# Gated activations turned in 32x32 squares by VectorE and regrouped through device memory, in a two-layer encoder on one core

## The chip, the cores and the metric

The kernel runs on one core of a Trainium2 chip. The metric is device time in microseconds (us), from the program's start to its end; lower is better. The median of three runs of the kernel before is 1835.18 us (1835.18 to 1835.51).

A core has a matrix engine (TensorE, rows named PE, with its weight loads under PEld), VectorE (DVE), ScalarE (ACT), GpSimd (POOL) and SyncE (SP), each with its own in-order queue of instructions, and 16 DMA engines. An instruction waits until its operands are there, and everything behind it on the same engine waits with it. SP here does nothing but issue DMAs; a DMA that must wait, for a buffer to come free or for data to be finished, holds up the DMAs behind it on SP.

## The reference, cut to what matters

Two layers; 512 tokens of width 1024, float32. Each layer holds two gated feed-forward blocks ("ffn" below, inner width 2816) with attention and convolution ("mix") between them:

```python
def swiglu(x, w_gate, w_up, w_down):
    return (jax.nn.silu(x @ w_gate) * (x @ w_up)) @ w_down

for l in range(DEPTH):
    x = x + 0.5 * swiglu(rms_norm(x, ffn1_norm[l]), ffn1_w_gate[l], ffn1_w_up[l], ffn1_w_down[l])
    ...  # h, attention and conv from x
    x = x + jnp.concatenate([attn, conv], axis=-1) @ w_out[l]
    x = x + 0.5 * swiglu(rms_norm(x, ffn2_norm[l]), ffn2_w_gate[l], ffn2_w_up[l], ffn2_w_down[l])
    x = rms_norm(x, post_norm[l])
```

The change touches the four ffn blocks only.

## The kernel before, in words

`x` stays on the chip with its features on the 128 partitions: `x[:, m, :]` holds features 128m to 128m+127 of all 512 tokens, for m = 0 to 7. Every float32 product is made of three matmuls of rounded halves: each operand is split into a high part (an ACT cast) and a low part (a DVE subtraction), and `mm3` adds high times high, high times low and low times high in a PSUM bank (lines 144 to 146). A bank holds 128 partitions x 512 float32.

An ffn goes through its 22 tiles of 128 inner features in six units (`UNITS` = 2, 4, 4, 4, 4, 4 tiles; unit 0 is `opening`, units 1 to 5 are `unit`). A unit of four tiles makes gate and up for all 512 tokens by a Strassen scheme with seven `product` calls of 24 matmuls each, in the order b11, b21, t2, t3, t1, t4, b22 (the names of the token-side operands). The weight sums that the scheme needs are made by DVE from loaded tiles (`add`, line 325), and the weights are split by line 227 (ACT) and line 229 (DVE). The results have tokens on the partitions. They are put together by `copied` and `join` (lines 341 and 346), and `gated` makes silu(gate) times up: an ACT instruction (line 355) and a DVE instruction (line 356) per 128 tokens, each 128x256.

The second matmul of the ffn, `down`, needs the inner features on the partitions. So `turned` transposes: four 128x128 TensorE transposes against an identity fill one bank with one tile of inner features for all 512 tokens (line 365), and `split` makes its high and low part from the bank (lines 150 and 151). There are two banks of that kind for `opening` and four for each unit. The `down` matmuls (96 for four tiles) of one unit are placed between the products of the next: `between(0)` turns, `between(1)` to `between(4)` take two of the eight output tiles each. `update` (line 443) adds half the bank to `x`. The last unit's activations are turned after the first matmuls of the last `down` groups, which also take unit 4's tiles.

The order of instructions on each engine is set by a scheduler at build time, which follows the program's order and its own estimates of durations; a DMA is placed in SP's order by the same scheduler. Buffers come from pools with a fixed number of places: `fr` 9 places for loaded gate and up weights (a unit uses 8), `raw` 3 for loaded `down` weights and two weight sums, `wh` and `wl` 4 each for split weights, `e` 4 for activations, `r` 40 (the "ring") for operands on the token side, PSUM 7 banks. `POOL` issues the few DMAs that add while they load (line 317), through a scratch area whose size `dynamic_dma_scratch_size` sets.

## Time and profile before

| | |
|---|---|
| median of three runs | 1835.18 us |
| the profiled execution's own time | 1836.73 us |
| its span, first to last instruction | 1834.9 us |
| mean granted TensorE clock | 0.993 |
| PE busy | 1793.2 us, 98% |
| DVE busy | 1347.8 us, 73% |
| ACT busy | 948.6 us, 52% |
| share of the 16 DMA engines taken by SP's queue | 28.6% |
| matmuls of line 365 (transposes) | 352 |

A row of a group gives line, engine, operation, output and inputs by name, shapes, count, then busy time in us and the mean duration of one in ns, then the engine's idle time just before and what ended it. In a timeline the first column is the start in us from the span's start, the second the time until the last of the row's instructions ends. A row of the windows view gives a stretch, its length, and for each engine the busy us with the number of instructions, then the granted clock, the share of DMA time and GB/s. Matmuls overlap, so the time that one takes from the next is read from the distance of their starts and not from a duration. The transposes of line 365 mark the four ffn blocks: they lie at about 38 to 319, 593 to 874, 940 to 1228 and 1502 to 1783 us.

### The profile page before, as it was taken

How to read it: one execution, taken by the hardware profiler on the slowest of the kernel's cores; microseconds unless marked ns; L12 is line 12 of the kernel's file. 1: busy time of each engine (PE TensorE's matmuls, PEld its weight loads, DVE VectorE, ACT ScalarE, POOL GpSimd, SP SyncE). 2: the span in 40 equal slices, each digit the busy share in tenths (PEclk: the TensorE clock that was granted, in tenths of full speed). 3: DMA queues.
4: the chain of work that ended last, by engine and by line, in shares of the span. 5: the costliest groups of instructions: out<-in, count | busy, mean ns of one | idle time of the engine just before them, and what ended most of it. 6: DMA issues, size and time to landing. Idle time of an engine off the chain costs nothing.

```text
span 1834.9 us, 22168 instructions
## 1 busy us (share of the span) xinstructions
PE 1793.2 (98%) x8512; PEld 1489.1 (81%) x8512; DVE 1347.8 (73%) x1803; ACT 948.6 (52%) x1471; POOL 279.0 (15%) x216
## 2 busy tenths in 40 slices
PE   8999999999999999999998999999999999999997
PEld 6888888888788888888877888888978788888885
DVE  8957876587957957866778667755988678577754
ACT  6534445467954634445644344444778455344442
POOL 4000000058931000000000000000688300000000
PEclk9999999999999999999999999999999999999998
DMA  8332322225134332322712332123250534323221
GB/s 294 107 123 89 117 70 69 92 87 136 25 127 106 108 123 93 105 99 69 229 66 92 107 103 92 69 71 112 76 149 1 164 89 126 115 81 115 69 70 58
DMA packets 58492, 187.95 MB, mean 102 GB/s; under 512 B 6033, under 2 KB 6417, under 8 KB 58385
## 3 DMA queue, kind: packets, MB, share of 16 engines
q1 hardware_dynamic: 54496, 173.56, 28.6%
q0 software_dynamic: 3456, 12.58, 3.9%
q8 instruction: 67, 1.10, 0.3%
q10 hardware_dynamic: 432, 0.38, 0.1%
q14 instruction: 41, 0.33, 0.1%
HBM read 184.40 MB, written 2.10 MB: 102 GB/s over the span
## 4 chain that ended last, share of the span: by engine, by line
PE 69%; issue 19%; DVE 7%; ACT 3%; POOL 2%; DMA 1%; SPq 0%; POOLq 0%; DVEq 0%; ACTq 0%
PE ps L144 21%; PE ps L146 21%; PE ps L145 20%; PE ps L752 2%; PE ps L365 1%; PE ps L718 1%; DVE wl L229 1%; ACT pr L795 1%; PE ps L739 1%; DVE fr L325 1%; DVE wl L139 1%; DVE cv L791 1%; POOL y L799 1%; POOL sck L162 0%; PE ps L182 0%
## 5 line engine op out<-in xcount | busy, mean ns | idle before, releaser
L144 PE MATMUL ps<-wh,r 128*128 128x512 f32 (+2 forms) x1392 | 525.2, 387 | 13.0 <-ACT wh L227 7.5
L145 PE MATMUL ps<-wl,r 128*128 128x512 f32 (+2 forms) x1392 | 534.5, 386 | 0.0
L146 PE MATMUL ps<-wh,r 128*128 128x512 f32 (+2 forms) x1392 | 532.1, 385 | 0.0
L227 ACT CAST wh<-fr 128x1024 fp32r<-128x1024 f32 x256 | 268.9, 1050 | 264.4 <-PE ps L146 141.3
L229 DVE TENSOR_TENSOR wl<-fr,wh 128x1024 fp32r<-128x1024 f32 x256 | 314.3, 1230 | 106.0 <-ACT wh L227 105.8
L146 PE MATMUL ps<-r,wl 128*128 128x512 f32 x1008 | 391.4, 389 | 0.5 <-POOL wl L139 0.5
L145 PE MATMUL ps<-r,wh 128*128 128x512 f32 x1008 | 391.4, 389 | 0.0
L144 PE MATMUL ps<-r,wh 128*128 128x512 f32 x1008 | 390.7, 393 | 0.3 <-ACT r L150 0.3
L144 PEld LDWEIGHTS ps<-wh,r 128*128 128x128 f32 x1392 | 262.4, 189 | 63.6 <-ACT wh L227 7.5
L145 PEld LDWEIGHTS ps<-wl,r 128*128 128x128 f32 x1392 | 262.5, 189 | 50.6 <-issue 0.5
L146 PEld LDWEIGHTS ps<-wh,r 128*128 128x128 f32 x1392 | 262.4, 188 | 50.2
L133 ACT CAST wh<-raw 128x1024 fp32r<-128x1024 f32 (+2 forms) x150 | 148.9, 997 | 217.8 <-issue 89.0
L146 PEld LDWEIGHTS ps<-r,wl 128*128 128x128 f32 x1008 | 189.2, 188 | 40.9 <-POOL wl L139 1.3
L145 PEld LDWEIGHTS ps<-r,wh 128*128 128x128 f32 x1008 | 189.2, 188 | 40.6 <-issue 1.4
L144 PEld LDWEIGHTS ps<-r,wh 128*128 128x128 f32 x1008 | 188.8, 188 | 40.9 <-ACT r L150 1.2
L139 DVE TENSOR_TENSOR wl<-raw,wh 128x1024 fp32r<-128x1024 f32 (+3 forms) x134 | 157.9, 1179 | 64.1 <-ACT wh L133 63.1
L162 POOL TENSOR_TENSOR rtok<-vtok,minus_half 128x4 f32<-128x4 f32 x9 | 11.1, 1230 | 1107.7 <-DVE vtok L188 1107.7
L443 DVE SCALAR_TENSOR_TENSOR x<-ps,x 128x512 f32<-128x512 f32 x128 | 88.2, 689 | 111.4 <-PE ps L146 110.7
L799 POOL TENSOR_TENSOR y<-y,pr 128x509 f32<-128x509 f32 (+15 forms) x120 | 157.7, 1316 | 50.2 <-ACT pr L795 42.9
L325 DVE TENSOR_TENSOR fr<-fr,fr 128x1024 f32<-128x1024 f32 x112 | 135.3, 1219 | 7.7 <-DMA fr<-in_wgu 7.2
L355 ACT ACTIVATE e<-e,rtok 128x256 f32<-128x256 f32 x120 | 61.0, 509 | 111.5 <-DVE e L346 111.2
L341 ACT COPY e<-ps 128x512 f32<-128x512 f32 x120 | 70.3, 587 | 64.1 <-PE ps L146 63.9
(165 smaller groups left out, 1731.9 us busy)
## 6 DMA issues: line engine op xcount, KB each, us to landing
fr<-in_wgu SPq DMA_DIRECT2D x176, 512.0 KB, 4.0
raw<-in_wd SPq DMA_DIRECT2D x64, 512.0 KB, 4.2
raw<-in_wd SPq DMA_DIRECT2D x32, 384.0 KB, 3.2
raw<-in_wcv SPq DMA_DIRECT2D x16, 512.0 KB, 3.3
raw<-in_wout SPq DMA_DIRECT2D x16, 512.0 KB, 3.7
raw<-in_wgu SPq DMA_DIRECT2D x8, 512.0 KB, 4.2
fr<-in_wgu POOLq DMA_DIRECT2D x8, 512.0 KB, 7.0
raw<-in_wgu POOLq DMA_DIRECT2D x8, 512.0 KB, 7.6
```

The lines of the kernel that those rows point to most:

```text
L133: A.copy(hi[:, :w], raw[:, :w])
L139: (G if kind in POOLW.split() else V).tensor_tensor(lo[:, :w], raw[:, :w], hi[:, :w].bitcast(FP), ALU.subtract)
L144: T.matmul(o, lh, rh, start=first, stop=False, skip_group_check=free)
L145: T.matmul(o, lh, rl, start=False, stop=False, skip_group_check=free)
L146: T.matmul(o, ll, rh, start=False, stop=last, skip_group_check=free)
L227: A.copy(hi[:, :w], src[:, :w])
L229: V.tensor_tensor(lo[:, :w], src[:, :w], hi[:, :w].bitcast(FP), ALU.subtract)
L325: V.tensor_tensor(oh, ah, bh, ALU.add)
L341: A.copy(w[:, j, :N], o[j][:, :N])
L355: A.activation(out[j][:, :h], src[j][:, :h], AF.Silu, scale=r)
L443: V.scalar_tensor_tensor(x[:, m, :], pd, 0.5, x[:, m, :], ALU.mult, ALU.add)
L799: order["conv"] = G.tensor_tensor(acc[:, s:], acc[:, s:], pr[:, s:], ALU.add).ins
```

## The change

The transposes on TensorE go away. What `gated` leaves, 128 tokens x 256 inner features, is turned by VectorE in squares of 32x32 (`turn`): one instruction takes a 128x256 tile and writes 128 x 8 x 32 into a block of 128 x 8 x 128. After it, partition 32a + i of the block holds, for each of eight groups of 32 inner features, feature i of the group for the 32 tokens of the a-th quarter of each 128. Two tiles of inner features for all 512 tokens fill one block, by four such instructions. `moved` then writes the block to device memory with four DMAs, one for each a (32 partitions, 256 runs of 512 bytes, 128 KB), and reads it back with two DMAs of 256 KB, one for each tile of inner features. The tokens of the tile that comes back stand in the order a, t, j instead of t, a, j. `down` works on them as they stand, and `update` reads its bank in the permuted order (t, a, j) to add it to `x`. The factor 0.5 of `update` is now in `rh`, half of the norm's factor, which `gated` multiplies in. `halved` makes the high part by an ACT cast from the tile read, and the low part in place by DVE.

A unit's blocks are moved in the order b1, b0, so the two halves of a unit's four tiles swap places, and the host puts the rows of the `down` weights in that order (`turns`). `moved` is called at the end of the unit in the program, `halved` where `turned` stood. `e` gets five places instead of four, the pool of one R tile one instead of two, and the scratch area is halved.

```diff
-WIDE = 4
+WIDE = 5
...
-    rpool = ctx.enter_context(tc.tile_pool(name="rp", bufs=2))
+    rpool = ctx.enter_context(tc.tile_pool(name="rp", bufs=1))
+    dram = ctx.enter_context(tc.tile_pool(name="dram", bufs=4, space=bass.MemoryType.DRAM))
...
         def gated(t, src, out, N):
             h = N // 2
             for j in range(2):
-                r = rt[0][:, 2 * t + j:2 * t + j + 1]
+                r, rh = (v[:, 2 * t + j:2 * t + j + 1] for v in rt)
                 A.activation(out[j][:, :h], src[j][:, :h], AF.Silu, scale=r)
-                V.scalar_tensor_tensor(out[j][:, :h], src[j][:, h:N], r, out[j][:, :h], ALU.mult, ALU.mult)
+                V.scalar_tensor_tensor(out[j][:, :h], src[j][:, h:N], rh, out[j][:, :h], ALU.mult, ALU.mult)
             return out
-        def turned(vs, N, act):
-            for b in range(len(vs)):
-                for i in range(N // 2 // P):
-                    ps = bank()
-                    for t in range(2):
-                        for j in range(2):
-                            T.transpose(ps[:, (2 * t + j) * P:(2 * t + j + 1) * P],
-                                        vs[b][t][j][:, i * P:(i + 1) * P], ident)
-                    act.append(split(ps))
+        def block():
+            return fpool.tile([P, 8, P], FP, tag="e", name=nm("e"), bufs=WIDE)
+
+        def turn(to, t, v):
+            for j in range(2):
+                V.transpose(to[:, :, (2 * t + j) * 32:(2 * t + j + 1) * 32], v[j][:, :HS])
+
+        def moved(blk):
+            away = dram.tile([2, P, S], FP, tag="d", name=nm("d"))
+            for a in range(4):
+                nc.sync.dma_start(
+                    out=away[:, :, a * P:(a + 1) * P].rearrange("f (b i) t -> i (f b) t", i=32),
+                    in_=blk[a * 32:(a + 1) * 32])
+            ds = []
+            for i in range(2):
+                d = slot(FR)
+                nc.sync.dma_start(out=d.bitcast(FP), in_=away[i])
+                ds.append(d)
+            return ds
+
+        def halved(d):
+            hi = slot(FR)
+            A.copy(hi, d.bitcast(FP))
+            V.tensor_tensor(d, d.bitcast(FP), hi.bitcast(FP), ALU.subtract)
+            return hi, d
...
         # opening
-            rt.append(norm())
-            vs = []
+            rt.extend((norm(), tiny("rh", NT)))
+            V.tensor_scalar(rt[1], rt[0], 0.5, None, ALU.mult)
+            blk = block()
             for t in range(2):
-                v = wide()
-                vs.append(gated(t, os[2 * t:2 * t + 2], [v[:, j, 0:HS] for j in range(2)], S))
-            return [vs]
+                v = tmp()
+                turn(blk, t, gated(t, os[2 * t:2 * t + 2], [v[:, j * HS:(j + 1) * HS] for j in range(2)], S))
+            return moved(blk)
...
         # unit
-            gated(0, a, a, N)
+            b0 = block()
+            turn(b0, 0, gated(0, a, a, N))
...
-            gated(1, d, d, N)
+            b1 = block()
+            turn(b1, 1, gated(1, d, d, N))
...
-            gated(0, c, c, N)
+            turn(b1, 0, gated(0, c, c, N))
+            b1 = moved(b1)
             product(bx, a12, "b22", False, True)
             s = tmp()
-            s = gated(1, bx, [s[:, j * HS:(j + 1) * HS] for j in range(2)], N)
-            return [[a, s], [c, d]]
+            turn(b0, 1, gated(1, bx, [s[:, j * HS:(j + 1) * HS] for j in range(2)], N))
+            return b1 + moved(b0)
 
         def update(m, pd):
-            V.scalar_tensor_tensor(x[:, m, :], pd, 0.5, x[:, m, :], ALU.mult, ALU.add)
+            xm = x[:, m, :].rearrange("p (t a j) -> p t a j", t=NT, a=4)
+            V.tensor_tensor(xm, pd.rearrange("p (a t j) -> p t a j", a=4, t=NT), xm, ALU.add)
...
                 if i == 0:
-                    turned(vs, S, acts)
+                    acts.extend(halved(d) for d in ds)
...
+    turns = np.arange(F).reshape(NF, P)
+    for f in range(UNITS[0], NF, 4):
+        turns[f:f + 4] = turns[[f + 2, f + 3, f, f + 1]]
...
-    nc = bacc.Bacc("TRN2", target_bir_lowering=False, num_devices=1, dynamic_dma_scratch_size=4096)
+    nc = bacc.Bacc("TRN2", target_bir_lowering=False, num_devices=1, dynamic_dma_scratch_size=2048)
```

How the order moves is shown at three places. In the rows below, line numbers of the changed kernel differ from those of the kernel before by one to a few tens, and the number behind a name tells tiles of one pool apart.

First DVE, at the passage from unit 3 to unit 4 of the first ffn, from the gating of c (e_1417, in the change e_1434) to the split of the first weight of product t2 (wl_1847, in the change wl_1868). Before, with the last gating instructions of unit 3 (line 356) between splits and sums of unit 4's weights:

```order
L356 SCALAR_TENSOR_TENSOR e_1417<-e_1417,rtok_326 128x256
L356 SCALAR_TENSOR_TENSOR t_1669<-ps_1232,rtok_326,t_1669 128x256
L325 TENSOR_TENSOR fr_1676<-fr_1676,fr_1684 128x1024
L229 TENSOR_TENSOR wl_1769<-fr_1678,wh_1767 128x1024
L356 SCALAR_TENSOR_TENSOR t_1669<-ps_1233,rtok_326,t_1669 128x256
L229 TENSOR_TENSOR wl_1773<-fr_1680,wh_1771 128x1024
L325 TENSOR_TENSOR fr_1678<-fr_1678,fr_1674 128x1024
L325 TENSOR_TENSOR fr_1680<-fr_1680,fr_1676 128x1024
L139 TENSOR_TENSOR wl_1809<-raw_1805,wh_1807 128x1024
L229 TENSOR_TENSOR wl_1847<-fr_1674,wh_1845 128x1024
L151 TENSOR_TENSOR r_1735<-ps_1729,r_1734 128x512
```

The same place in the change, without its first rows:

```order
L326 TENSOR_TENSOR fr_1718<-fr_1718,fr_1726 128x1024
L230 TENSOR_TENSOR wl_1787<-fr_1720,wh_1785 128x1024
L366 STREAM_TRANSPOSE e_1578<-e_1434 128x8x32
L366 STREAM_TRANSPOSE e_1395<-t_1700 128x8x32
L357 SCALAR_TENSOR_TENSOR t_1700<-ps_1271,rh_330,t_1700 128x256
L230 TENSOR_TENSOR wl_1791<-fr_1722,wh_1789 128x1024
L326 TENSOR_TENSOR fr_1720<-fr_1720,fr_1716 128x1024
L366 STREAM_TRANSPOSE e_1395<-t_1700 128x8x32
L140 TENSOR_TENSOR wl_1827<-raw_1823,wh_1825 128x1024
L326 TENSOR_TENSOR fr_1722<-fr_1722,fr_1718 128x1024
L230 TENSOR_TENSOR wl_1868<-fr_1716,wh_1866 128x1024
L230 TENSOR_TENSOR wl_1872<-fr_1718,wh_1870 128x1024
```

The transposes of unit 3 stand among the splits that unit 4's first products need, and the second split for t2 has moved up next to the first.

Second SP, at the same passage. Before, it has loads alone:

```order
L315 DMA fr_1682<-in_wgu 128x1024
L315 DMA fr_1684<-in_wgu 128x1024
L131 DMA raw_1805<-in_wd 128x2x512
L315 DMA fr_1686<-in_wgu 128x1024
L315 DMA fr_1688<-in_wgu 128x1024
L315 DMA fr_2134<-in_wgu 128x1024
L131 DMA raw_1880<-in_wd 128x2x512
L315 DMA fr_2136<-in_wgu 128x1024
```

In the change:

```order
L316 DMA fr_1730<-in_wgu 128x1024
L316 DMA fr_2180<-in_wgu 128x1024
L372 DMA d_1659<-e_1578 32x8x128 x4
L378 DMA r_1664<-d_1659 128x512
L378 DMA r_1666<-d_1659 128x512
L372 DMA d_1707<-e_1395 32x8x128 x4
L132 DMA raw_1901<-in_wd 128x2x512
L316 DMA fr_2182<-in_wgu 128x1024
L378 DMA r_1712<-d_1707 128x512
L378 DMA r_1714<-d_1707 128x512
L316 DMA fr_2184<-in_wgu 128x1024
```

The writes of the blocks (d) and the reads of the tiles (r) stand in the one queue with the weight loads; the reads of the second block stand behind a load of `down` weights and the second load for unit 5 (fr_2182).

Third PE, at the end of the first ffn, where unit 5's activations are taken. Before, after the twelve matmuls of the third output tile (ps_2478) on unit 4's activations:

```order
L146 MATMUL ps_2478<-r_2221,wl_2474 128x512
L365 MATMUL ps_2515<-cst,e_2186 128x128 x2
L365 MATMUL ps_2515<-cst,t_2453 128x128 x2
L365 MATMUL ps_2524<-cst,e_2186 128x128 x2
L365 MATMUL ps_2524<-cst,t_2453 128x128 x2
L365 MATMUL ps_2533<-cst,e_2303 128x128 x2
L365 MATMUL ps_2533<-cst,e_2340 128x128 x2
L365 MATMUL ps_2542<-cst,e_2303 128x128 x2
L365 MATMUL ps_2542<-cst,e_2340 128x128 x2
```

In the change, after the twelve matmuls of a fourth output tile (ps_2642):

```order
L147 MATMUL ps_2642<-r_2244,wl_2640 128x512
L145 MATMUL ps_2526<-r_2565,wh_2510 128x512
L145 MATMUL ps_2527<-r_2565,wh_2516 128x512
L145 MATMUL ps_2528<-r_2565,wh_2522 128x512
L145 MATMUL ps_2642<-r_2565,wh_2638 128x512
L146 MATMUL ps_2526<-r_2456,wh_2510 128x512
```

The 16 transposes are gone, and 48 matmuls instead of 36 on unit 4's activations stand ahead of the first on unit 5's (r_2565 and r_2456 are high and low part of its first tile); of its third tile the first stands 17 matmuls later.

12 lines of the change are left out of this document (6 added, 6 removed).

## The prediction

> **What bounds the kernel now.** I read the page's first part, its chain, the windows view by stage, and then the groups of line 365.
>
> ```profile
> PE 1793.2 (98%) x8512; PEld 1489.1 (81%) x8512; DVE 1347.8 (73%) x1803; ACT 948.6 (52%) x1471; POOL 279.0 (15%) x216
> PE 69%; issue 19%; DVE 7%; ACT 3%; POOL 2%; DMA 1%; SPq 0%; POOLq 0%; DVEq 0%; ACTq 0%
> core 0: us, PE busy (x) PEld busy (x) DVE busy (x) ACT busy (x) POOL busy (x), PEclk, DMA share, GB/s
> 20.00:93.00 73.00, 72.36 (x336) 59.87 (x335) 70.55 (x95) 42.74 (x64) 8.02 (x7) 1.00 0.53 159
> 93.00:113.00 20.00, 20.00 (x90) 16.57 (x89) 7.46 (x9) 7.23 (x9) 0.00 (x0) 1.00 0.36 106
> 600.00:640.00 40.00, 39.27 (x181) 32.23 (x181) 38.56 (x52) 23.77 (x35) 0.00 (x0) 1.00 0.31 100
> 960.00:1000.00 40.00, 34.92 (x154) 28.28 (x153) 38.39 (x52) 19.12 (x28) 0.00 (x0) 0.96 0.32 99
> 1510.00:1550.00 40.00, 39.29 (x182) 32.24 (x181) 38.51 (x51) 23.79 (x35) 0.00 (x0) 1.00 0.32 99
> 250.00:275.00 25.00, 25.00 (x115) 20.65 (x114) 22.54 (x27) 11.99 (x16) 0.00 (x0) 1.00 0.24 85
> 213.00:274.66 61.66, 61.66 (x282) 51.23 (x281) 46.12 (x53) 27.82 (x36) 0.00 (x0) 1.00 0.28 94
> ```
>
> PE is busy 98% of the span and carries 69% of the chain. The rows of windows split the ffn in two. In a steady unit (213 to 274.66) PE has no idle time at all and DVE 61.66 - 46.12 = 15.5 us of it, so PE sets the pace. At the starts of the four ffn blocks (the rows from 20, 600, 960 and 1510 us) DVE is busy 96 to 97% and PE has small gaps: the two are about equally full, and DVE is the one that holds. Behind the start (93 to 113) DVE drops to 7.46 us of 20. The end of a steady unit (250 to 275) is a dense place for DVE too: 2.46 us free in 25.
>
> **What is removed.** How much a transpose takes from PE is read from the distance of starts:
>
> ```profile
> 316.27 0.39 PE L144 MATMUL ps<-r,wh 128*128 128x512 f32 x1
> 316.50 0.39 PE L145 MATMUL ps<-r,wh 128*128 128x512 f32 x1
> 316.72 0.39 PE L146 MATMUL ps<-r,wl 128*128 128x512 f32 x1
> 316.95 0.38 PE L365 MATMUL ps<-cst,e 128*128 128x128 f32 x2
> ...
> 317.83 1.04 PE L365 MATMUL ps<-cst,e 128*128 128x128 f32 x8
> 318.62 0.94 PE L144 MATMUL ps<-r,wh 128*128 128x512 f32 x3
> 319.40 0.39 PE L145 MATMUL ps<-r,wh 128*128 128x512 f32 x1
> L365 PE MATMUL ps<-cst,e 128*128 128x128 f32 x272 | 44.3, 273 | 3.2 <-DVE e L356 1.7 <-issue 1.5
> L365 PE MATMUL ps<-cst,t 128*128 128x128 f32 x80 | 16.6, 272 | 0.0
> ```
>
> Matmuls start 0.227 us apart. From the first of 16 transposes (316.95) to 319.40 are 2.45 us, of which three matmuls take 0.68: 1.77 for 16, 0.11 each. The steady unit agrees: 264 matmuls x 0.227 + 1.77 = 61.7 us against a width of 61.66. All 352 (272 + 80) are gone from the changed order, so that the change does what it says is settled: 352 x 0.11 = **38.7 us** less PE work. The Trainium skill, in "TensorE: Matmul & The Clock Gate", Part 4 (PE-mode transpose), gives about 275 ns for a transpose within a kernel; the rows above agree with that as a duration (273), but taken as a price it would make 97 us of 352 transposes, and the starts show that they overlap.
>
> Of the 38.7 us not all can arrive. The 8 transposes of the opening and the 16 taken in unit 2 lie in the stretches where DVE holds; PE arriving earlier there only waits. I count 24 x 4 x 0.11 = 10.6 us as not arriving, and 28.2 us from the other 64 per block.
>
> **What is added to DVE.** A 128x256 STREAM_TRANSPOSE stands in no trace here. The nearest rows:
>
> ```profile
> L356 DVE SCALAR_TENSOR_TENSOR e<-e,rtok 128x256 f32<-128x256 f32 x120 | 57.3, 479 | 13.9 <-ACT e L355 13.9
> L742 DVE COPY r<-ps 128x256 f32<-128x256 f32 x16 | 6.5, 408 | 0.0
> L742 DVE COPY r<-ps 128x512 f32<-128x512 f32 x16 | 10.9, 681 | 0.2 <-PE ps L739 0.2
> 268.22 0.48 DVE L356 SCALAR_TENSOR_TENSOR t<-ps,rtok,t 128x256 f32<-128x256 f32 x1
> 268.62 1.22 DVE L325 TENSOR_TENSOR fr<-fr,fr 128x1024 f32<-128x1024 f32 x1
> ```
>
> Instructions of 128x256 last 0.41 to 0.48 us and start 0.40 apart (268.22 to 268.62); one of 128x512 lasts 0.68, and by the same 0.08 takes 0.60. As bounds I take 0.33 (a copy's 0.41 less 0.08) and 0.60 (every element moved twice); as value 0.40, since it is one pass over 256 elements like the copy. The Trainium skill, in "VectorE: DVE Perf Modes", The three transpose paths, gives 311 ns for 128x128 of bf16; no run here shows it. An estimate from that page, twice the columns at twice the time, is 0.62 us, and the time would be that of the second rival below.
>
> There are 176, 44 per block. In the dense end of a unit stand six of them (two each for d, c and the last pair): 6 x 0.40 = 2.4 us in 2.46 us of free time. The product t2, the first that they can delay, now comes behind the whole of b21. So nothing is lost there, and nothing is left over either. Were the cover gone, each 0.1 us more per instruction would cost 0.6 us at each of 16 unit ends.
>
> At the starts there is no such room. Twelve (opening 4, unit 1 8) add 4.8 us; free are 73 - 70.55 = 2.45, 40 - 38.56 = 1.44, 1.61 and 1.49 us, so DVE comes 2.35 + 3.36 + 3.19 + 3.31 = 12.2 us later in sum.
>
> **The way through device memory.** SP issues four writes and two reads per block, 264 DMAs more.
>
> ```profile
> out_T<-r SPq DMA_DIRECT2D x8, 256.0 KB, 2.2
> rg<-in_rgain ACTq DMA_DIRECT2D x1, 64.0 KB, 6.0
> L960 SPq DMA_DIRECT2D out_T<-r x8: 332/332/348, 1826.8 to 1831.4; - x8
> SPq L315 <- DVE wl L229: 689.2, 137, 27.5
> L355 ACT ACTIVATE t<-ps,rtok 128x256 f32<-128x256 f32 x40 | 18.9, 473 | 18.7 <-PE ps L146 18.7
> L229 DVE TENSOR_TENSOR wl<-fr,wh 128x1024 fp32r<-128x1024 f32 x256 | 314.3, 1230 | 106.0 <-ACT wh L227 105.8
> L139 DVE TENSOR_TENSOR wl<-raw,wh 128x768 fp32r<-128x768 f32 x38 | 40.9, 1078 | 7.8 <-ACT wh L133 7.7
> L150 ACT CAST r<-ps 128x512 fp32r<-128x512 f32 x96 | 50.3, 600 | 54.5 <-PE ps L365 41.1 <-PE ps L770 13.5
> L151 DVE TENSOR_TENSOR r<-ps,r 128x512 fp32r<-128x512 f32 x96 | 60.5, 683 | 35.9 <-ACT r L150 35.9
> L443 DVE SCALAR_TENSOR_TENSOR x<-ps,x 128x512 f32<-128x512 f32 x128 | 88.2, 689 | 111.4 <-PE ps L146 110.7
> L759 DVE TENSOR_TENSOR t<-ps,rs 128x512 f32<-128x512 f32 x8 | 5.5, 686 | 3.6 <-PE ps L752 3.6
> ```
>
> Less the 0.08 us, a long split takes 1.13 to 1.15 us and a short one (128x768) 0.87 to 1.0. An issue takes 0.33 us on SP. A transfer lands after 2.2 us (256 KB stored) to 6.0 (the only one in runs of 512 bytes, at the crowded beginning); I take 2.2, the only store, in a quiet time like here.
>
> At the **end of an ffn**, from the last matmul of b22: ACT's silu 0.47, gating 0.40, a weight split 1.13 that stands between, the turn 0.40, four issues 1.3, the write 2.2, a read's issue 0.3 and landing 2.2, cast and subtraction 1.2: 9.6 us, or 17 at 6.0 per hop. The cover is 48 + 17 matmuls, 65 x 0.227 = 14.7 us: nothing lost, or 2.5 us four times. In a **steady unit** the activations are first used after b11, b21 and t2, 72 matmuls or 16.3 us, so the way is hidden in either case. The reads there wait on SP behind fr_2182, which needs a buffer that t2's split frees; but the loads in SP wait for DVE anyway (689.2 us in the row above) and were issued a unit ahead, so what stands behind the writes is not yet needed.
>
> In **unit 2** it is tighter. Between the last turn of b1 and the first subtraction of `halved`, DVE has 5.9 us of other work (two joins, one short and two long splits, two gatings, two turns); the way there takes four issues, a hop, three issues of the next block, a hop, one cast: 7.3 us. The subtraction holds DVE for about 1.4 us, with splits and updates of unit 2 behind it: 5.6 us in four blocks. With the 12.2 above, DVE is 17.8 us late at the starts. What reaches PE of it lies between none (operands ready ahead of use) and all; I take half, **8.9 us**.
>
> The rest costs nothing: cast and subtraction only change their source from a bank to the on-chip memory; `update` stays a 128x512 instruction from a bank (line 443 0.689 us; line 759, which reads a bank through a four-dimensional pattern, 0.686); the one R place and the smaller scratch area serve transfers that lie hundreds of us apart or four at a time.
>
> **The sum**, on the profiled execution: 1836.73 - 38.7 + 10.6 + 8.9 = 1817.5. That execution is 1.55 us above the median of the runs, so **1816 us**.
>
> **The rivals.**
>
> *All of it arrives.* DVE's lateness is absorbed: the scheduler has rearranged the starts, the 22 banks per block that transposes took are free, and the 10.6 us come too. For it: PE is 98% busy, and at 600 and 1510 it misses only 0.7 us. Against: DVE is full just there. 1836.7 - 38.7 - 1.55 = 1796.5.
>
> *The turn is dear, and the kernel slower.* At 0.60 us the dense ends overflow: 6 x 0.60 - 2.46 = 1.14 us at 16 unit ends, 18.2 us, and 12 x 0.2 x 4 = 9.6 us at the starts; t2's product waits for its split. 1817.5 + 27.8 - 1.55 = 1844. The sign turns where 48(t - 0.40) + 16(6t - 2.46) = 19.2, at t = 0.54 us. Against it: no DVE row of that size takes over 0.40 between starts.
>
> *The way is long, and the kernel slower.* At 6.0 us per hop the subtractions hold DVE 7.6 us longer in unit 2, 30 us in four blocks, and the ends lose 10: 1856. The sign turns near 4.6 us per hop. For it: 512-byte runs, write before read; against it the 2.2 us.
>
> **How the numbers follow.** Forecast 0.60, all arrives 0.18, dear turn 0.13, long way 0.09. The forecast's own range is 1807 to 1825 (none or all of the 17.8 us). Low end 1797, where the first rival lies; high end 1842, near the dear turn, for some 2 in 10 outside. About 0.2%, 3.7 us, is what a measurement can tell from no change. Faster: 0.56 of the forecast, 0.18, and 0.03 of milder turns, 0.77; same 0.06; slower 0.17.
>
> **What would show it.** The steady unit should shrink from 61.66 to 59.9 us with PE never idle; STREAM_TRANSPOSE should last near 0.48 with DVE still under 90% there; starts should show PE waiting for DVE splits by some us each; the first matmuls on unit 5's activations should not wait. The prediction is wrong if steady units show PE gaps before t2, if a d write or r read lands much later than 2.2 us, or if DVE sits waiting for DMA.

## The result and the profile after

The changed kernel takes 1818.58 us in the median of four runs (1818.25 to 1821.34), the kernel before 1835.18 us beside it (1834.08 to 1835.51): a ratio of 0.9914, 95% interval 0.9897 to 0.9931. The profiled execution of the changed kernel took 1818.46 us, its span is 1816.7 us, and its granted clock 0.993 as before. The forecast was 1816 us, its range 1797 to 1842.

The page's first part, and the windows view of a steady unit, of the dense end of a unit and of the four starts, as shown of the kernel before:

```profile
PE 1761.6 (97%) x8160; PEld 1448.8 (80%) x8160; DVE 1405.7 (77%) x1983; ACT 949.7 (52%) x1471; POOL 280.1 (15%) x216
core 0: us, PE busy (x) PEld busy (x) DVE busy (x) ACT busy (x) POOL busy (x), PEclk, DMA share, GB/s
213.00:272.89 59.89, 59.89 (x266) 49.60 (x265) 47.72 (x62) 27.53 (x36) 0.00 (x0) 1.00 0.41 132
250.00:275.00 25.00, 25.00 (x112) 20.69 (x111) 22.71 (x31) 11.19 (x15) 0.00 (x0) 1.00 0.27 92
20.00:93.00 73.00, 67.05 (x287) 53.46 (x286) 68.37 (x98) 38.88 (x56) 9.33 (x8) 0.98 0.54 163
600.00:640.00 40.00, 37.47 (x161) 29.49 (x161) 37.55 (x55) 22.35 (x32) 0.00 (x0) 1.00 0.30 100
960.00:1000.00 40.00, 35.83 (x154) 28.75 (x155) 35.88 (x53) 17.76 (x26) 0.00 (x0) 1.00 0.39 125
1510.00:1550.00 40.00, 37.50 (x159) 29.26 (x160) 34.64 (x50) 18.11 (x27) 0.00 (x0) 1.00 0.45 147
```

A steady unit now fits into 59.89 us with PE never idle and DVE at 47.72 (80%); before it took 61.66. Three of the four starts have gone the other way: from 20 to 93 us PE has 5.95 us of idle time where it had 0.64, and at 600 and 1510 it has 2.5 us where it had 0.7. At 960 PE had more than a small gap before: 5.08 us of idle time in 40 at a granted clock of 0.96, now 4.17 at 1.00. DVE has idle time in all four: it is not simply full, it waits too.

What was added, from the groups by line (count | busy us, mean ns | idle before and what ended it) and the DMAs (count, size, median us to landing):

```profile
L366 DVE STREAM_TRANSPOSE e<-e 128x256 f32<-128x256 f32 x120 | 52.2, 439 | 0.6
L366 DVE STREAM_TRANSPOSE e<-t 128x256 f32<-128x256 f32 x56 | 23.0, 424 | 0.0
L467 DVE TENSOR_TENSOR x<-ps,x 128x512 f32<-128x512 f32 x128 | 86.5, 686 | 44.1 <-PE ps L147 43.7
L385 DVE TENSOR_TENSOR r<-r,r 128x512 fp32r<-128x512 f32 x88 | 58.4, 682 | 70.7 <-ACT r L384 70.5
L384 ACT CAST r<-r 128x512 fp32r<-128x512 f32 x88 | 53.2, 618 | 81.3 <-DMA r<-d 80.3
...
d<-e SPq DMA_DIRECT2D x176, 128.0 KB, 2.7
r<-d SPq DMA_DIRECT2D x88, 256.0 KB, 4.0
```

A turn lasts 0.42 to 0.44 us, and two rows of DVE's timeline give what it takes from the next instruction: four turns start at 40.40 and the next instruction at 41.73, 0.33 each.

```profile
40.40 1.42 DVE L366 STREAM_TRANSPOSE e<-t 128x256 f32<-128x256 f32 x4
41.73 1.19 DVE L230 TENSOR_TENSOR wl<-fr,wh 128x1024 fp32r<-128x1024 f32 x1
```

The write lands after 2.7 us, the read after 4.0. ACT stands 80.3 us in front of casts (line 384) whose tile has not come back, and DVE 70.5 us behind ACT. Part of PE's waits is for what stands behind these; the first rows are from the waits view, those below them from the timelines of ACT and PE in the first block's unit 1. (The longest wait of line 145 for line 228, 7.7 us, is in front of the kernel's first matmul; before the change it was 7.5.)

```profile
PE ps L145 <- ACT wh L228: 8.5, 5, 7.7
PE ps L147 <- DVE r L158: 7.1, 6, 2.0
PE ps L145 <- ACT r L157: 5.9, 3, 2.8
PE ps L145 <- DVE e L347: 4.5, 4, 2.0
...
PE ps L145 <- ACT r L384: 1.8, 5, 0.4
```

```profile
49.68 0.62 ACT L384 CAST r<-r 128x512 fp32r<-128x512 f32 x1 [1.74 <-DMA r<-d]
50.21 0.51 ACT L356 ACTIVATE e<-e,rtok 128x256 f32<-128x256 f32 x1
50.62 0.60 ACT L384 CAST r<-r 128x512 fp32r<-128x512 f32 x1
51.13 0.62 ACT L157 ACTIVATE r<-r 128x512 fp32r<-128x512 f32 x1
...
51.80 0.50 PE L145 MATMUL ps<-wh,r 128*128 128x512 f32 x1 [2.83 <-ACT r L157]
```

ACT waits for the opening's first tile to come back (the cast at 49.68), and behind it in ACT's order stands the operand that product t2 needs (line 157). PE loses 2.83 us, although the opening's activations themselves are not multiplied before unit 2.

Where the time went is shown best by numbering the 7200 matmuls of the three-matmul lines in each trace and subtracting the start of the n-th before from that of the n-th after. "Starts" is what this lag gains (below zero) or loses over the 480 matmuls at the beginning of each of the four blocks (opening, unit 1 and most of unit 2), "rest" all else; the last two columns hold to about 0.2 us. The same is given for every run below:

```
us against before             block 1   2     3     4   starts   rest    total
the change                      5.0   2.5   0.1   2.3     9.9  -28.4    -18.4
1  opening, unit 1 on TensorE  -0.4  -1.0   0.0  -0.3    -1.7  -27.2    -28.9
2  opening's halves later       4.7   2.1  -1.4   3.0     8.5  -26.6    -18.1
3  no device memory             1.4  -2.0  -4.7  -2.0    -7.2  -28.0    -35.3
4  no turn                     -0.3  -3.1  -6.2  -3.0   -12.6  -27.3    -39.9
5  turn twice                  10.9  12.3   7.8   8.4    39.3   26.2     65.5
6  two hops                     9.0  10.9   7.7  10.9    38.5   62.9    101.3
7  way on POOL's queue          6.2   9.8   6.4   6.6    29.0  -21.8      7.2
8  opening on TensorE           1.9   0.6  -1.8   1.3     2.0  -27.6    -25.6
9  down loads on POOL           2.9   3.3   3.1   2.1    11.5  -23.4    -11.9
10 as 1, down loads on POOL    -0.5  -0.9   0.2   0.0    -1.1  -20.0    -21.2
11 as 5, down loads on POOL    11.8  12.7   9.2  12.3    46.0   45.0     91.0
12 as 2, four raw places        6.4   2.3   1.1   3.2    13.0  -27.2    -14.2
```

So the change gained 28.4 us where 28.2 was forecast, and lost 9.9 at the starts, where the forecast had a loss of 8.9. Why the starts lose is what most of the experiments ask.

### The profile page after: what moved, and what is told of

Same layout as the page of the kernel before. It is cut to its first block, busy times and chain, and to the rows that moved or that the text cites. A ratio compares the mean times of both kernels' runs of the same rounds, so it can differ in the third digit from the quotient of the medians.

```text
span 1816.7 us, 22175 instructions
## 1 busy us (share of the span) xinstructions
PE 1761.6 (97%) x8160; PEld 1448.8 (80%) x8160; DVE 1405.7 (77%) x1983; ACT 949.7 (52%) x1471; POOL 280.1 (15%) x216
## 4 chain that ended last, share of the span: by engine, by line
PE 65%; issue 19%; DVE 5%; DMA 3%; ACT 3%; POOL 1%; SPq 1%; POOLq 0%; DVEq 0%; ACTq 0%
PE ps L145 20%; PE ps L147 20%; PE ps L146 20%; PE ps L775 2%; PE ps L741 1%; DVE wl L230 1%; DMA fr<-in_wgu 1%; ACT pr L818 1%; DMA r<-d 1%; PE ps L762 1%; DMA d<-e 1%; DVE fr L326 1%; ACT r L747 1%; POOL sck L163 0%; PE ps L201 0%
## 5 line engine op out<-in xcount | busy, mean ns | idle before, releaser
L467 DVE TENSOR_TENSOR x<-ps,x 128x512 f32<-128x512 f32 x128 | 86.5, 686 | 44.1 <-PE ps L147 43.7
L385 DVE TENSOR_TENSOR r<-r,r 128x512 fp32r<-128x512 f32 x88 | 58.4, 682 | 70.7 <-ACT r L384 70.5
```

What stands on the lines that cost most here:

```text
L385: V.tensor_tensor(d, d.bitcast(FP), hi.bitcast(FP), ALU.subtract)
L467: V.tensor_tensor(xm, pd.rearrange("p (a t j) -> p t a j", a=4, t=NT), xm, ALU.add)
```

## The experiments

Times are medians of four runs each, the ratio is to the kernel before on the same chip. One caution holds for all: the scheduler orders each kernel anew, so an edit can also move instructions that it doesn't name.

### 1. Opening and unit 1 turned by TensorE again

```diff
-                if i == 0:
+                if i == 0 and u < 3:
+                    turned(ds, S, acts)
+                elif i == 0:
                     acts.extend(halved(d) for d in ds)
...
             gated(0, a, a, N)
+            if not first:
+                b0 = block()
+                turn(b0, 0, a)
```

> The change is undone for the opening and unit 1 of each block alone: their six tiles of inner features are turned by TensorE again (24 transposes per block, in units 1 and 2), unit 2's sums into x read their bank in plain order, and units 2 to 5 keep the change. Main theory (the starts of the blocks, full on DVE, lose about 10 us in sum to the turned opening and unit 1, while the other 64 transposes per block bring 64 x 4 x 0.11 = 28.2 us): 1835.2 - 28.2 = 1807, and a trace without the PE waits for r (lines 157 and 158) near the starts. Rival (the loss at the starts is from something else that the change did: one place for the R tile, five places of e, halved scratch area): the starts stay slow and the 24 transposes come back only where PE waits anyway, 1818 to 1819.

1808.28 us (1807.53 to 1810.45), ratio 0.9854, 0.9840 to 0.9869. As the main theory said. The start loss is gone (-1.7 in the table), and the rest gains 27.2 us by itself. Of PE's waits within the blocks only two kinds of more than 2 us are left, both there before the change as well; lines 157 and 158 no longer appear:

```profile
PE ps L145 <- ACT wh L228: 7.6, 1, 7.6
PE ps L145 <- DVE e L347: 4.0, 1, 4.0
```

The one R place, the five places of e and the smaller scratch area are still in this kernel, so they don't make the loss. It is the fastest kernel of this study that computes the reference, faster than both the kernel before and the change: its interval lies wholly below that of the change (0.9897 to 0.9931).

### 2. The opening's cast and subtraction moved to unit 2

```diff
-                if i == 0:
-                    acts.extend(halved(d) for d in ds)
+                if i == 0 and u == 1:
+                    held.extend(ds)
+                elif i == 0:
+                    acts.extend(halved(d) for d in (held + ds if u == 2 else ds))
```

> One call is moved: the cast and subtraction of the opening's two tiles stand at unit 2's between(0), beside unit 1's four, instead of at unit 1's. The work of every engine is the same. Theory A (at the starts ACT and DVE, in order, stand behind the reads from device memory, with the operands for t2 and t3 behind them): the PE waits for r of lines 157 and 158 shrink, two to three us in each of two to four blocks, 1810 to 1814. Theory B (the starts lose because 12 turns of about 0.35 us are added to a DVE that is full there): the same work in another order, 1817 to 1820.

1817.45 us (1814.48 to 1818.81), ratio 0.9900, 0.9885 to 0.9915: by the median what theory B said. The table hides that theory A was right about unit 1: in the first block the lag at matmul 240 falls from 7.1 to 1.5 us. But at matmul 360 it is 4.9 in both kernels. The loss came back at the start of unit 2. The timelines of ACT and PE there:

```profile
84.76 0.83 ACT L134 CAST wh<-raw 128x768 fp32r<-128x768 f32 x1 [4.52 <-DMA raw<-in_wd]
85.50 1.99 ACT L228 CAST wh<-fr 128x1024 fp32r<-128x1024 f32 x2
...
86.59 0.73 PE L145 MATMUL ps<-wh,r 128*128 128x512 f32 x2 [1.94 <-ACT wh L228]
88.13 0.79 PE L146 MATMUL ps<-wl,r 128*128 128x512 f32 x1 [0.81 <-DVE wl L230]
88.72 0.63 PE L147 MATMUL ps<-wh,r 128*128 128x512 f32 x1
89.15 0.63 PE L145 MATMUL ps<-wh,r 128*128 128x512 f32 x1
```

ACT waits 4.52 us for a down load, two weight casts stand behind it, and PE behind those. After the wait the matmuls start 0.43 us apart (88.72, 89.15) instead of 0.227, thirteen of them until 94.25: 2.6 us more than the waits themselves.

### 3. No way through device memory, and 4. no turn

The third kernel leaves the regrouping out (and puts the low part in a place of its own in the ring instead of over the tile read), the fourth the turn. What comes out of either is not the reference's.

```diff
 # 3
-            away = dram.tile([2, P, S], FP, tag="d", name=nm("d"))
...
-            return ds
+            return [blk[:, 4 * i:4 * i + 4, :].rearrange("p b t -> p (b t)") for i in range(2)]
 # 4, in gated; the calls of V.transpose go
-                V.scalar_tensor_tensor(out[j][:, :h], src[j][:, h:N], rh, out[j][:, :h], ALU.mult, ALU.mult)
+                V.scalar_tensor_tensor(to[:, :, (2 * t + j) * 32:(2 * t + j + 1) * 32],
+                                       src[j][:, h:N].rearrange("p (b i) -> p b i", i=32), rh,
+                                       out[j][:, :h].rearrange("p (b i) -> p b i", i=32), ALU.mult, ALU.mult)
```

> The way through device memory is left out: the cast and the subtraction read the turned block on the chip as it stands, so the features are not regrouped and what comes out is not the reference's. Turns, casts, subtractions and everything else stay. Theory A (waits in order behind the reads): the 10 us lost at the starts mostly come back, 1808 to 1812. Theory B (DVE's added work): 1816 to 1819, since the turns stay. In steady units neither expects a difference, since PE has no idle time there with the way either.

> The turns are left out: the gating instruction writes its result into the block directly, unturned, so what comes out is not the reference's. The way through device memory stays. 176 DVE instructions of about 0.35 us fewer, 12 of each block's 44 at its start. Theory B (DVE's added work at the starts): half of 12 x 0.35 x 4 = 17 us comes back, 1809 to 1812. Theory A (waits behind the reads): only the writes start 0.35 us earlier, 1817 to 1818. In steady units neither expects a gain, since PE is never idle there.

1800.34 us (1798.41 to 1802.17), ratio 0.9809, 0.9794 to 0.9824, and 1796.97 us (1794.14 to 1797.84), ratio 0.9787, 0.9771 to 0.9804. Leaving the way out brings 18.2 us, leaving the turn out 21.6, and nearly all of it at the starts (the "rest" is 28.0 and 27.3, as in the change). Neither theory stands alone: A said 1817 to 1818 for the fourth run, B 1816 to 1819 for the third. PE's waits, of the fourth kernel and then of the third:

```profile
PE ps L145 <- ACT wh L228: 7.5, 1, 7.5
PE ps L145 <- DVE e L347: 5.1, 3, 3.1
```

```profile
PE ps L145 <- DVE e L347: 5.9, 2, 4.1
...
PE ps L147 <- DVE r L158: 1.7, 2, 1.0
```

Line 157 is gone in both, line 158 in the fourth. In the fourth kernel the way is still there and ACT waits 82.1 us for reads, but of PE's waits only one, of 0.8 us, is put down to the casts behind them. In the third the turns are still there: 176 of them at 0.33 us are 58 us of DVE time, and the kernel is 3.4 us slower than the fourth by the medians, at the starts 5.4 us by the table. Against the change, leaving out the turn gives the starts 22.5 us and leaving out the way 17.1. The two sum to far more than there is to win, so they are not two separate prices: most of the loss needs both. A reading that fits the traces is a sum of delays on in-order engines: DVE's turns make a write late, the write a read, the read holds ACT and DVE, and these hold the operands and weights of the next product. A kernel without either was not run, so what the way costs alone is not known.

The fourth run also speaks of the 24 transposes per block that the prediction counted as not arriving. DVE's work there is what it was before the change (1348.6 us against 1347.8), and the starts gain 12.6 us, more than the 10.6. But by blocks it is 0.3, 3.1, 6.2 and 3.0 against 2.65 each. In the second and fourth blocks, where DVE was 96% busy before, the gain arrives in full. In the first and third PE does wait for DVE. PE's timeline in the first block of the fourth kernel, and then in the third block of the kernel before:

```profile
62.82 0.50 PE L145 MATMUL ps<-wh,r 128*128 128x512 f32 x1 [1.81 <-DVE e L347]
```

```profile
968.93 0.66 PE L144 MATMUL ps<-wh,r 128*128 128x512 f32 x1 [4.01 <-DVE e L346]
```

In the first block the wait, and matmuls that start 0.43 us apart behind it, take back most of the gain. In the third more arrives than was taken away, because waits that were there before shrink or go: the 4.01 us (3.10 in the fourth kernel), and 1.53 and 1.06 us in front of transposes. So a DVE that is 96 to 97% busy holds PE in two of the four starts and not in the other two.

### 5. Every turn twice, and 6. a second hop

```diff
 # 5
+                for _ in range(2):
                     V.transpose(to[:, :, (2 * t + j) * 32:(2 * t + j + 1) * 32], v[j][:, :HS])
 # 6
+            again = dram.tile([2, P, S], FP, tag="d2", name=nm("d2"))
+            for i in range(2):
+                nc.sync.dma_start(out=again[i], in_=away[i])
...
-                nc.sync.dma_start(out=d.bitcast(FP), in_=away[i])
+                nc.sync.dma_start(out=d.bitcast(FP), in_=again[i])
```

> Each STREAM_TRANSPOSE is issued twice in a row to the same place: 176 DVE instructions of about 0.36 us more, 12 at each block's start, 6 at each dense unit end. Theory D (at the starts what DVE gets more reaches PE in full; in steady units DVE work has room): 12 x 0.36 x 4 = 17 us more, 1834 to 1838, and steady units of 59.9 us unchanged. The prediction's rule for a dear turn (0.72 us per pair: dense ends overflow by 6 x 0.72 - 2.46 = 1.9 us at 16 ends, and half of the 17 us at the starts): 30 + 9 us more, about 1857.

> A second hop is put between write and read: the block is copied once more inside device memory (two DMAs of 256 KB), then read from the copy. By the rows of the change a write lands after 2.7 us and a read after 4.0, so the way gets 3 to 5 us longer and SP gets 88 more issues. Steady units: hidden (72 matmuls, 16.3 us, against a way of some 10 us, then 14), no difference. Theory A (at starts and in unit 2 ACT and DVE stand behind the reads): 3 to 5 us more in unit 1 or 2 of each block and up to 2 us at each block's end, 1830 to 1842. Theory D (only DVE's added work counts): 1817 to 1822.

1901.24 us (1897.42 to 1902.55), ratio 1.0354, 1.0337 to 1.0372, and 1942.18 us (1931.83 to 1946.96), ratio 1.0577, 1.0541 to 1.0613. Both far above every expectation, and most of it not at the starts: 29.4 and 28.6 us more than the change there, and 54.6 and 91.3 us more in the rest. The waits of PE in the fifth kernel, and its timelines of ACT and PE at a steady unit:

```profile
PE ps L145 <- ACT r L385: 51.9, 15, 7.3
PE ps L145 <- ACT r L157: 16.4, 4, 7.2
```

```profile
239.10 1.04 ACT L134 CAST wh<-raw 128x1024 fp32r<-128x1024 f32 x1 [9.00 <-DMA raw<-in_wd]
...
243.69 1.14 ACT L385 CAST r<-r 128x512 fp32r<-128x512 f32 x2
...
244.37 2.07 PE L145 MATMUL ps<-r,wh 128*128 128x512 f32 x4 [7.28 <-ACT r L385]
```

Here the casts of unit 3's first two tiles (line 385 in this kernel) stand behind a down weight that ACT waited 9.00 us for, and PE waits 7.28. In the change itself the casts of the first two tiles stand ahead of such a load and those of the last two, the later block, behind it, and these just fit. Its ACT timeline:

```profile
226.40 1.05 ACT L134 CAST wh<-raw 128x1024 fp32r<-128x1024 f32 x1 [5.03 <-DMA raw<-in_wd]
227.35 0.91 ACT L356 ACTIVATE e<-e,rtok 128x256 f32<-128x256 f32 x2
228.16 1.04 ACT L228 CAST wh<-raw 128x1024 fp32r<-128x1024 f32 x1
229.10 1.14 ACT L384 CAST r<-r 128x512 fp32r<-128x512 f32 x2
```

The first high part of unit 3's later block is ready 1.10 us before the matmul that takes it starts. In the eight transitions of this kind (from unit 2 to 3 and 3 to 4 of four blocks) that room is 0.50 to 1.43 us; from unit 4 to 5 it is over 22 us, since those activations are used only at the block's end. So the way of the later block was not hidden with 7 us to spare, as the prediction's 9.6 us in 16.3 would have it, but with about one, although its cover is longer: its first matmul (230.81) stands not 72 but 90 matmuls, 20.4 us, behind the last of b22 (210.41). The first two tiles, needed after 72, keep 5.8 to 5.9 us.

The DMA engines have a part in this that no run separates. In the fifth kernel SP issues the down load at 231.20, so nearly all of ACT's wait is its transfer: it lands 7.8 us after its issue, and the loads and writes issued up to 235.8 take 7.3 to 8.5. The DMA share is 1.00 from 237 to 240 us. In the change the load is issued at 220.12 and lands 6.2 us later, and the share is 1.02 and 0.93 in the two stretches of 3 us from 220; before the change, in the same place of the same unit, it was 0.00 and 0.72.

Of the sixth kernel PE's largest wait is for such casts too:

```profile
PE ps L145 <- ACT r L387: 67.7, 16, 6.4
```

### 7. The way on POOL's queue

```diff
-                nc.sync.dma_start(
+                G.dma_start(
                     out=away[:, :, a * P:(a + 1) * P].rearrange("f (b i) t -> i (f b) t", i=32),
...
-                nc.sync.dma_start(out=d.bitcast(FP), in_=away[i])
+                G.dma_start(out=d.bitcast(FP), in_=away[i])
```

> All 264 DMAs of the way through device memory are issued from POOL's queue instead of SP's, where loads of weights stand behind writes that wait for turns. Theory C (the starts lose because loads on SP come late behind those writes; without them on SP 18 us came back): 1800 to 1808. Theory D or A (DVE's added work, or the reads' own duration): 1815 to 1820, later still if an issue takes longer from POOL than the 0.33 to 0.46 us on SP.

1843.78 us (1840.48 to 1846.71), ratio 1.0048, 1.0033 to 1.0063. Theory C is not borne out: SP's queue is free of the way, and all is slower, at the starts by 19.1 us and by 6.6 in the rest. But the run changes more than the order. An issue takes 0.56 to 0.58 us on POOL instead of 0.35 to 0.46 on SP (medians), and writes and reads land later from POOL's queue, 3.0 and 5.0 us in the median instead of 2.7 and 4.0:

```profile
d<-e POOLq DMA_DIRECT2D x176, 128.0 KB, 3.0
r<-d POOLq DMA_DIRECT2D x88, 256.0 KB, 5.0
```

So it is a second test of a longer way, with the same sign as the second hop, and a gain from the order alone could be hidden in it.

### 8. The opening alone turned by TensorE

```diff
+                if i == 0 and u == 1:
+                    turned(ds, S, acts)
+                elif i == 0:
                     acts.extend(halved(d) for d in ds)
```

> The change is undone for the opening alone: its two tiles are turned by TensorE (8 transposes per block, 8 x 0.11 x 4 = 3.5 us) and put into the permuted token order while they are split from the bank; unit 1 and all later units keep the change, so the DVE has 4 turns per block fewer and the opening has no way through device memory. If the opening's read and turns make the loss at the starts (ACT waits 1.7 us for that read, PE 2.8 us behind it): 1807 to 1811. If unit 1's eight turns and the reads taken in unit 2 make it: 1817 to 1822.

1811.82 us (1810.28 to 1812.48), ratio 0.9873, 0.9858 to 0.9888. Between the two expectations, nearer the first. PE has 3.5 us of transposes more than in the change, and the starts are still 7.9 us better. Against starts at which all savings arrive, the change loses 9.9 + 10.6 = 20.5 us and this kernel 2.0 + 7.0 = 9.0 (16 transposes per block fewer than before are worth 7.0 in the four blocks). So the opening's two tiles make somewhat more than half of the loss, unit 1's four the rest.

### 9, 10 and 11. The down loads on POOL's queue

In the change (9), in the kernel of the first run (10) and in that of the fifth (11):

```diff
-                w = load_w(wd[l, m, :, f0 * P:(f0 + n) * P], n * P)
+                w = load_w(wd[l, m, :, f0 * P:(f0 + n) * P], n * P, by=G)
...
-        nc.sync.dma_start(out=to.rearrange("p (m c) -> p m c", m=2) if two else to, in_=src)
+        (by or nc.sync).dma_start(out=to.rearrange("p (m c) -> p m c", m=2) if two else to, in_=src)
```

> The change, with the loads of the down weights issued from POOL's queue, so that they no longer stand on SP behind writes that wait for turns. Theory C' (on SP the down weights come late, ACT stands behind them for 69.6 us in sum, and the casts of the activations behind ACT): ACT's waits for those loads shrink to under a third, the starts lose less, 1803 to 1812. Theory D (the starts are short of DVE time, and the queue of those loads makes no difference to DVE): 1815 to 1820.

> Opening and unit 1 turned by TensorE as in the first run, with the down weights from POOL's queue in addition. PE waits for little but what it waited for before the change, so both theories expect the first run's 1808 within 2 us; a lower time would show that waits in units 2 to 5 were left there, a higher one that the loads are slower from POOL's queue.

> Every turn twice as in the fifth run, with the down weights from POOL's queue. If the 52 us that PE waited there in steady units for casted activations came from the order of SP's queue (a down load behind writes that wait for a turn, ACT behind that load, the casts behind ACT): most of the 52 us goes, 1840 to 1860. If the way itself (turn, write, read) is too long for its cover by then: 1890 to 1905.

1825.61 us (1821.49 to 1825.81), ratio 0.9943, 0.9928 to 0.9958; 1813.37 us (1812.13 to 1816.56), ratio 0.9879, 0.9863 to 0.9896; 1928.31 us (1925.87 to 1929.47), ratio 1.0506, 1.0491 to 1.0522. Every one is slower than its counterpart, by 7, 5 and 27 us. Issued from POOL the down loads land about as soon after their issue (512 KB: 4.1 us in the median of the ninth kernel, 4.5 in the change), and still ACT's waits for them grow from 69.6 to 85.8 us. So the order of SP's queue alone does not make the down weights late, and theory C' falls.

```profile
ACT wh L134 <- DMA raw<-in_wd: 85.8, 25, 5.2
```

In the eleventh kernel POOL issues a down load at 232.79, 0.4 us after DVE ended the split of the load before (231.16, 1.22 us long), and POOL's wait ahead of it is put down to that split. What its issue waits for is a place of `raw`, which DVE gives free, and DVE has its turns to do between the splits. The larger part comes after that: this load lands 9.0 us after its issue.

### 12. Run 2 with a fourth place of raw

```diff
-                raw = wpool.tile([P, WC], FP, tag="raw", name=nm("raw"), bufs=3)
+                raw = wpool.tile([P, WC], FP, tag="raw", name=nm("raw"), bufs=4)
...
-    tmps = ctx.enter_context(tc.tile_pool(name="tmps", bufs=5))
+    tmps = ctx.enter_context(tc.tile_pool(name="tmps", bufs=4))
...
-    nc = bacc.Bacc("TRN2", target_bir_lowering=False, num_devices=1, dynamic_dma_scratch_size=2048)
+    nc = bacc.Bacc("TRN2", target_bir_lowering=False, num_devices=1, dynamic_dma_scratch_size=1024)
```

> The second run's edit (the opening's cast and subtraction beside unit 1's in unit 2) and a fourth place for loaded down weights, raw; the room comes from one place of temporaries fewer (four instead of five) and a scratch area of 1024. In the second run all loss lay at the start of unit 2: ACT stood 4.5 to 5.0 us behind a down load that SP issued only when DVE had split the load before it, PE stood 2.8 to 4.1 us behind ACT and DVE, and 10 to 13 matmuls after that started 0.43 us apart instead of 0.227. Theory R (the place that comes free late is the cause): about 4 x 4 = 16 us less than the second run, 1801 to 1805. Rival W (the reads from device memory, 3.7 to 4.1 us late there too, would hold ACT the same): 1813 to 1818.

1820.90 us (1820.13 to 1823.32), ratio 0.9918, 0.9901 to 0.9934. Theory R's cause was there, but taking it away gains nothing: in unit 2's beginning ACT no longer waits for down loads, and now the casts of activations come last. From the waits view of PE and the timeline of ACT:

```profile
PE ps L145 <- ACT r L384: 13.4, 11, 1.9
```

```profile
99.13 0.62 ACT L384 CAST r<-r 128x512 fp32r<-128x512 f32 x1 [4.87 <-DMA r<-d]
```

This is rival W in part, and a little worse than it said. Of the 13.4 us, 1.9 in each block are for the opening's casts (93.12 in the first), in front of which ACT waits for no read; most of the rest stands behind the reads. PE's waits for DVE's splits (line 230) grow as well, from 4.4 to 7.2 us. Whether the room that was given up for it (a place of temporaries, half the scratch area) adds to the time was not tried.

## Why the prediction was right

**The likeliest case came, with its sum within 3 us, but two of its terms were wrong and cancelled, and that was luck.** By steps:

*38.7 us of PE work, 28.2 of them outside the starts.* Right. The rest gained 28.4 us in the change, and 26.6 to 28.0 in runs 1 to 4 and 8. A steady unit shrank by 1.77 us, to the 59.9 that was named, and 16 transposes at 0.11 us are 1.77.

*10.6 us not arriving, because DVE holds at the starts.* Wrong in sum. With DVE's load as before (run 4) the starts gain 12.6 us. The busy share of 96 to 97% that I read as DVE holding does not tell whether PE waits for it: at 600 and 1510 PE was busy 39.27 and 39.29 us of 40, and there the saving arrives; at 960, with the same share of DVE, PE was busy 34.92 at a clock of 0.96, which I passed over as a small gap. Only in the first block, with 0.3 of 2.65 us, did it go as I said.

*8.9 us, half of DVE's 17.8 us of lateness.* Wrong in size, and the choice of half was a guess between none and all. The turns, with the way in place, cost the starts 22.5 us (9.9 against -12.6), more than all of the 17.8. The two terms miss in opposite directions: 10.6 + 8.9 = 19.5 us were forecast between the whole saving and the result, and 20.5 (9.9 + 10.6) measured, but as -2.0 and 22.5. That is why the sum came out. A sum that is right shows its total, not its terms; only the fourth run separated them.

*The turn at 0.40 us.* Good: 0.33 to 0.36 between starts, 0.42 to 0.44 as a duration where near 0.48 was expected. The dense unit ends hold it, DVE busy 22.71 us of 25. The estimate from the Trainium skill, 0.62 us, worked out from "VectorE: DVE Perf Modes", The three transpose paths, is too high for this shape; its 128x128 of bf16 is in no run here.

*The way, 2.2 us per hop, hidden behind 72 matmuls.* The outcome was right, the reason too generous. The hops are 2.7 and 4.0 us. What was missing altogether is what stands in line between them. Gatings and turns wait in DVE's order behind splits, and writes behind turns. Reads come after the next block's writes, casts after a down weight that lands late while the DMA engines are full. By the traces a unit's first two tiles have 5.8 to 5.9 us left of 16.3, its last two 0.5 to 1.4 of 20.4. With turns or hops doubled the kernel is far slower than before (runs 5 and 6), and with writes and reads that land 0.3 and 1.0 us later (run 7) slightly slower. Both rivals for the slower side named a real mechanism, dear turn and long way, and both priced it too low: for a pair of turns at 0.72 us the rule gives 1857 and the run 1901. The prediction had the steady units hidden even at 6.0 us per hop; with one hop more the rest of the blocks takes 91 us longer than in the change.

*The subtraction that holds DVE in unit 2, 5.6 us.* Right in kind: in unit 2 DVE stands behind ACT's casts. But the opening's tiles, which I passed over, do the same in unit 1: there ACT stands 1.74 us and PE 2.83, and run 8 gives the opening more than half of the loss.

*The ends of the blocks, nothing lost.* Nearly: the first part of unit 5's later tiles is ready 0.05 to 0.26 us before its matmul in the four blocks, and at 873.9 PE had to wait about half a microsecond.

*The rest costs nothing.* Right: `update` takes 0.686 us (0.689 before), and in run 1 the pools and the scratch area stand as in the change with no loss at the starts.

*What would show it.* Two of the signs named as proof against the prediction did appear, reads later than 2.2 us and DVE waiting behind DMA (70.5 us), without making it wrong. In the steady units that wait was idle time of engines that had some to give.

*All of it arrives* did not happen, though run 4 shows that its 1796.5 us is the price without a turn: 1796.97.

Open in part is how the 22.5 us divide between the turns' own DVE time (48 x 0.33 = 16 us at the four starts) and the later writes that they cause. Run 3 has the turns without the writes, and its starts are 5.4 us behind those of run 4; so some 17 us come only where the way is there too, unless the other place of the low part in run 3 changes more than it seems. Open too is whether another order of the start could keep the change and lose nothing; runs 2, 7, 9 and 12 tried four, and none gained more than its spread.

## What to carry to other kernels

The busy shares of two nearly full engines do not tell which one binds: ask for which of the two the other waits, stage by stage, before writing off a saving or charging a cost to the end. A way that is "hidden" needs its whole line costed, with everything that stands in order between its steps on each engine it passes and what else is on the DMA engines just then, and then the room that is left. Here that was about 1 us, and two small additions to it cost 83 and 124 us. When the part of a change that hurts is confined to one stage, do the change where the room is: turning only units 2 to 5 gained 10 us more than turning all.

## What the runs showed of the hardware

A wait of PE can cost more than itself. After many of the waits of 2 to 7 us the matmuls of this kernel start 0.43 us apart for up to 14 of them, before they return to 0.227. The windows view of the fifth kernel shows it as granted clock (the last column but two of a row):

```profile
core 0: us, PE busy (x) PEld busy (x) DVE busy (x) ACT busy (x) POOL busy (x), PEclk, DMA share, GB/s
244.37:250.50 6.13, 6.13 (x15) 4.78 (x15) 3.81 (x6) 1.70 (x3) 0.00 (x0) 0.50 0.51 193
250.50:256.50 6.00, 6.00 (x28) 4.97 (x27) 0.69 (x1) 0.59 (x1) 0.00 (x0) 1.00 0.00 0
```

For 6.13 us after the wait the clock is 0.50 and the row counts 15 matmuls, the last of which starts at its end; then it is 1.00, with 28 in 6.00 us. The 14 before that would take 14 x 0.227 = 3.18 us at the full rate, so this wait cost about 2.9 us more than itself, and part of what runs 5 and 6 lost beyond their waits is this. The Trainium skill, in "TensorE: Matmul & The Clock Gate", Part 1, has the clock fall to half after at least one idle window of about 3.4 us and come back after at least one as long busy one. The half rate agrees, and so do the 6.13 us that it lasted; the idle window is not borne out: here an idle stretch of 1.94 us followed after two matmuls by one of 0.81 (run 2, 86.59 and 88.13), and one of 2.83 us in the change (eight matmuls, 1.5 us), were enough, and not every wait of that length was followed by it (2.14 us at 750.25 in run 5 was not).

The other surprise is the DMA queue of POOL: the same writes and reads issued there take 0.56 to 0.58 us to issue instead of 0.35 to 0.46 and land, counted from the start of the issue, 0.3 and 1.0 us later than from SP, and the whole kernel is 25 us slower.
